# The last chunk pair of a ConvFFN's up projection as a block product, and the border to the down projection laid out anew

## The chip, the cores and the metric

The kernel runs on one core of one Trainium2 chip. Its engines run side by side and wait for one another by semaphores: PE (TensorE, the matrix multiplier), DVE (VectorE), ACT (ScalarE), POOL (GpSimd) and SP (SyncE, which here only issues DMAs). The metric is the device time of one execution in microseconds (us), as the median of several runs.

## The reference

One layer of a streaming encoder on 1024 positions plus 16 meta tokens, width 1024, all in float32. The work around the change is its last part, a gated feed-forward with a causal convolution of width 3, and a final norm:

```python
def _conv_ffn(xn, w_up, conv_w, conv_b, w_down):
    hid = xn @ w_up                       # (1040, 1024) @ (1024, 5632)
    hp = jnp.pad(hid, ((0, 0), (CONV_WIDTH - 1, 0), (0, 0)))
    conv = conv_b + sum(hp[:, j:j + seq_len] * conv_w[j] for j in range(CONV_WIDTH))
    val, gate = jnp.split(conv, 2, axis=-1)
    return (jax.nn.silu(gate) * val) @ w_down   # (1024, 2816) @ (2816, 1024)
```

## The kernel before

Every float32 operand of a matmul is held as two tiles, a rounded high part and the low rest. A cast (ACT, from raw to high) and a split (raw minus high, on DVE or POOL, the helper at line 137) make them, and each product is three matmuls: high by high, high by low, low by high.

**Up.** The hidden width of 2816 is 22 chunks of 128 (NFF); for each chunk c there is a gate chunk and a value chunk of weights, so a chunk pair. The normed input lies transposed in `xhi` and `xlo` (128 partitions, 8 rows of K, 1040 columns). Pairs 0, 1, 2 and 21 are *plain* (`plain_steps`, line 1339): for each half three pieces of about 342 columns, each 24 matmuls into one bank, then the convolution straight from the bank (ACT line 1361, DVE line 1363). Pairs 3 to 20 are *block pairs* (`block_pair`, line 1490): the four quarters of weights and input are combined to seven products in place of eight (`seven`, line 217). `weight_forms` makes the combined weights (POOL sums at line 1451, casts at 1304, splits at 137), and the combined inputs T1 to T4 stand in the pool `tforms` (the list `T`). A block pair reads B11, B21 and B22 of `xhi` and `xlo` and the four forms, in the order A11 B11, S2 T2, A12 B21, S3 T3, S1 T1, A22 T4, S4 B22, each in two pieces of 258 and 256 columns and 12 matmuls a piece. The quarter B12 is read only when the forms are made. A block pair's result goes through `hg` and `hv` (three buffers `h` in pool `hid`), and then through the convolution (ACT line 1501, DVE line 1503, twice for each half). `glue` (line 1311) does silu on ACT, the product of gate and value (POOL, for the last pair DVE), and the store to `a_d` in HBM.

**Down.** The product of `a_d` with `w_down` is made in the same seven-product way from 11 pairs of rows j, in four groups: (8, 9), (7, 0, 1), (2, 3, 4), (5, 6, 10). Each group runs seven products p in the order 0, 4, 1, 2, 5, 3, 6 (the last group differs), each over four row tiles, with three matmuls of 512 columns for each j. `forms(p, j)` (line 1561) loads a tile of weights (`wr`) and a tile of rows (`ar`), casts both and splits both, on POOL for p = 0, 4 and 5 and on DVE otherwise, into an operand slot from the list `ops`. p = 4, 5 and 6 accumulate in the banks of 0, 1 and 3, after these have been copied out (lines 1702 to 1707). The sums stand in `u2` and in the rows `hs`, whose first four tiles are loaded with the residual (`h_load`).

**The border.** The plain pair 21 needs no T forms, so their pool is closed before it, and down's first pool `down1` (operand slots, raw buffers `a00` to `a11` and eight weight buffers `w`) takes its bytes while the plain pair runs. When the up stage's pools close (`st_r`: weights ring, hidden rows, outputs), the second pool `down` takes theirs: `gfB`, raw buffers, `u2`, `hs`, two more slots. A tile that takes used bytes waits until the last reader of them is done.

What sets the order: the program is traced, and a scheduler at build time sets for each engine one fixed order of instructions, by readiness in its own model and program order. `after(a, b)` adds an edge that places a behind b. Each engine, and each engine's DMA queue, then works in its order; an instruction that waits holds everything behind it on its engine.

## Time and profile before

| | us |
|---|---|
| three runs | 1425.33, 1426.13, 1426.46 (median 1426.13) |
| the profiled execution | 1427.24 |
| its span, from the first to the last instruction | 1425.5 |
| block pairs c = 3 to 20 | 824.3 to 1183.9 |
| plain pair c = 21 | 1183.9 to 1206.6 |
| down, TensorE | 1206.6 to 1417 |
| last evictions, norm and stores | 1417 to 1425.5 |

Times inside the profile count from the first instruction. The profile gives for each engine its busy time, and for each instruction its start, its duration and what ended the idle time before it. A matmul's duration includes its way through the array, which the next matmul overlaps, so that TensorE's pace is read from start to start.

### The profile page before, as it was taken

How to read it: one execution, taken by the hardware profiler on the slowest of the kernel's cores; microseconds unless marked ns; L12 is line 12 of the kernel's file. 1: busy time of each engine (PE TensorE's matmuls, PEld its weight loads, DVE VectorE, ACT ScalarE, POOL GpSimd, SP SyncE). 2: the span in 40 equal slices, each digit the busy share in tenths (PEclk: the TensorE clock that was granted, in tenths of full speed). 3: DMA queues.
4: the chain of work that ended last, by engine and by line, in shares of the span. 5: the costliest groups of instructions: out<-in, count | busy, mean ns of one | idle time of the engine just before them, and what ended most of it. 6: DMA issues, size and time to landing. Idle time of an engine off the chain costs nothing.

```text
span 1425.5 us, 26319 instructions
## 1 busy us (share of the span) xinstructions
PE 1410.6 (99%) x9607; PEld 1336.1 (94%) x9607; DVE 1070.3 (75%) x2048; ACT 709.0 (50%) x1381; POOL 764.2 (54%) x872
## 2 busy tenths in 40 slices
...
PEclk9999999999999999999999999999999999999999
...
GB/s 298 176 203 147 160 106 133 172 119 31 53 156 161 127 111 57 23 287 267 216 161 124 73 114 183 183 173 177 178 142 113 98 79 258 327 205 133 129 94 118
DMA packets 93318, 216.17 MB, mean 152 GB/s; under 512 B 14802, under 2 KB 22610, under 8 KB 92804
## 3 DMA queue, kind: packets, MB, share of 16 engines
...
HBM read 170.88 MB, written 71.71 MB: 170 GB/s over the span
## 4 chain that ended last, share of the span: by engine, by line
PE 95%; DMA 2%; issue 1%; ACT 1%; DVE 0%; POOL 0%; POOLq 0%; DVEq 0%; SPq 0%
PE mm L174 5%; PE mm L176 5%; PE mm L175 5%; PE sp L236 4%; PE sp L237 4%; PE sp L238 4%; PE tp L236 3%; PE tp L237 3%; PE tp L238 3%; PE mm L238 3%; PE mm L236 3%; PE mm L237 3%; PE po L966 3%; PE tp L920 2%; PE mm L1699 2%; PE mm L1698 2%
## 5 line engine op out<-in xcount | busy, mean ns | idle before, releaser
L174 PE MATMUL mm<-xhi,whi 128*128 128x342 f32 (+2 forms) x480 | 156.1, 325 | 0.0
L175 PE MATMUL mm<-xlo,whi 128*128 128x342 f32 (+2 forms) x480 | 155.4, 324 | 0.0
L176 PE MATMUL mm<-xhi,wlo 128*128 128x342 f32 (+2 forms) x480 | 154.6, 322 | 0.5 <-DMA wlo<-in_w_g_dram 0.5
L1313 POOL TENSOR_TENSOR ov<-ov,og 128x1024 f32<-128x1024 f32 x21 | 50.8, 2421 | 119.7 <-ACT og L1312 117.4
L137 DVE TENSOR_TENSOR sw<-sf,sw 128x512 fp32r<-128x512 f32 x72 | 73.4, 1020 | 46.2 <-ACT sw L1304 45.1
L1304 ACT CAST sw<-sf 128x512 fp32r<-128x512 f32 x72 | 44.9, 624 | 108.9 <-POOL sf L1451 80.1
L176 PEld LDWEIGHTS mm<-xhi,wlo 128*128 128x128 f32 x480 | 90.4, 188 | 1.3 <-DMA wlo<-in_w_g_dram 0.8
L174 PEld LDWEIGHTS mm<-xhi,whi 128*128 128x128 f32 x480 | 90.4, 188 | 1.1 <-issue 0.6
L175 PEld LDWEIGHTS mm<-xlo,whi 128*128 128x128 f32 x480 | 90.4, 188 | 0.4
L1451 POOL TENSOR_TENSOR sf<-raw,sf 128x512 f32<-128x512 f32 x36 | 62.9, 1748 | 38.8 <-DVE sw L137 38.7
L1451 POOL TENSOR_TENSOR sf<-raw 128x512 f32<-128x512 f32 x36 | 49.1, 1363 | 60.0 <-ACT ov L1361 21.5
L238 PE MATMUL mm<-xhi,sw 128*128 128x258 f32 (+1 forms) x288 | 81.0, 281 | 0.0
L236 PE MATMUL mm<-xhi,sw 128*128 128x258 f32 (+1 forms) x288 | 80.8, 280 | 0.0
L237 PE MATMUL mm<-xlo,sw 128*128 128x258 f32 (+1 forms) x288 | 80.7, 280 | 0.0
L883 ACT ACTIVATE pt<-pt,mx 128x400 f32<-128x400 f32 (+5 forms) x72 | 53.1, 737 | 45.2 <-DVE mx L876 44.9
L1503 DVE SCALAR_TENSOR_TENSOR ov<-hv,cwt,ov 128x1024 f32<-128x1024 f32 x36 | 69.9, 1942 | 0.4 <-ACT ov L1501 0.4
L885 POOL TENSOR_SCALAR pt<-pt,mx 128x400 f32<-128x400 f32 (+5 forms) x72 | 51.8, 721 | 33.3 <-DVE mx L884 28.3
L1304 ACT CAST sw<-raw 128x512 fp32r<-128x512 f32 x70 | 43.0, 621 | 45.0 <-PE sp L238 23.1
L137 DVE TENSOR_TENSOR sw<-raw,sw 128x512 fp32r<-128x512 f32 x70 | 57.9, 831 | 4.3 <-ACT sw L1304 4.0
L137 DVE TENSOR_TENSOR tl<-tp,th 128x512 fp32r<-128x512 f32 (+1 forms) x80 | 50.7, 634 | 12.2 <-ACT th L923 11.6
L923 ACT CAST th<-tp 128x512 fp32r<-128x512 f32 (+1 forms) x80 | 43.4, 543 | 32.1 <-PE tp L920 22.7
L852 POOL CAST qz<-q 64x128 fp32r<-64x128 f32 (+1 forms) x72 | 20.2, 283 | 67.2 <-PE sp L871 65.7
...
## 6 DMA issues: line engine op xcount, KB each, us to landing
raw<-in_w_up_dram SPq DMA_DIRECT2D x44, 512.0 KB, 3.7
t_d<-in_w_dn_dram POOLq DMA_DIRECT2D x44, 256.0 KB, 6.9
wr<-t_d SPq DMA_DIRECT2D x44, 256.0 KB, 3.4
ar<-a_d SPq DMA_DIRECT2D x41, 256.0 KB, 5.3
a_d<-ov SPq DMA_DIRECT2D x18, 512.0 KB, 2.6
wr<-in_w_dn_dram SPq DMA_DIRECT2D x33, 256.0 KB, 3.8
t_d<-in_w_dn_dram SPq DMA_DIRECT2D x22, 256.0 KB, 4.3
t_d<-t_d SPq DMA_DIRECT2D x22, 256.0 KB, 4.7
```

The lines of the kernel that those rows point to most:

```text
L137: return eng.tensor_tensor(out_, src, hi.bitcast(F), ALU.subtract)
L174: yield PE.matmul(ps, whi[:, i, :], ahi[:, i], start=(i == 0), stop=False)
L175: yield PE.matmul(ps, whi[:, i, :], alo[:, i], start=False, stop=False)
L176: yield PE.matmul(ps, wlo[:, i, :], ahi[:, i], start=False, stop=(i == k - 1))
L236: PE.matmul(ps, a[0][:, i], bh, start=(i == 0 and not joins), stop=False, skip_group_check=True)
L237: PE.matmul(ps, a[0][:, i], bl, start=False, stop=False, skip_group_check=True)
L238: PE.matmul(ps, a[1][:, i], bh, start=False, stop=(i == kh - 1), skip_group_check=True)
L883: ends[:] = rd, S.activation(pt[:n, :kc], pt[:n, :kc], AF.Exp, bias=low, scale=-1.0, accum_out=nm[:n, 0:1])
L885: sc_.append(GP.tensor_scalar(pt[:n, :kc], pt[:n, :kc], nm[:n, 1:2], 1.0, ALU.mult, ALU.mult))
L1304: S.copy(hi, src)
L1451: sums.append(GP.tensor_tensor(f_, a, b, op))
L1503: V.scalar_tensor_tensor(out=o, in0=h_[:, j:SEQ + j], scalar=cwc(j, m), in1=o, op0=ALU.mult, op1=ALU.add)
```

## The change

Chunk pair 21 becomes a block pair like those before it. Since it reads the T forms, their pool now lives through it, and down's first tiles are placed by when bytes come free:

- a small pool `down0`, taken before the forms, holds two weight buffers, two raw buffers `a00` and the constant `eps`; the slots of p = 0 are the quarter B12 of `xhi` and `xlo`;
- `down1` takes the bytes of the forms, whose tiles are laid out in the order of their last use (T2, T3, T1, T4): six weight buffers, `a01`, two slots (p = 4), `a10`, `a11`, `hs` 0 to 3, `u2`; p = 1 and 2 take quarters (0, 0) and (1, 0) as slots;
- `down` takes the bytes of the up stage: `gfB`, the raw buffers of every second pair of rows, `hs` 7 and 6, two slots (p = 5), two more (p = 6), `hs` 5 and 4; p = 3 takes quarter (1, 1).

The convolution of pair 21 (`conv_pair`) is now traced behind down's first product. Edges set the order at the border: the loads of group 0 in a chain behind the last up weights, pair 20's store behind the eighth of them, the `hs` loads behind the sixteenth; casts of p = 0 behind the pair's copies of c1, of p = 4 ahead of the first evictions, of p = 6 behind p = 1's evictions; the gate half of the convolution behind p = 1's splits and the value half behind p = 2's; p = 4's additions behind the gate half. The last pair's store is issued by POOL's queue in place of ACT's, and its outputs take the usual output buffers in place of the hidden rows' buffers.

```diff
--- before.py
+++ after.py
@@ -211,6 +211,8 @@
             los.append(split_lo(V, dlo[:, 4 * hf:4 * hf + 4, col:col + n], t3[:, :, :n], ho))
         return los
 
+    kept = {}
+
     def m_ps():
         return pp.tile([P, 512], F, tag="mm", name="mm", bufs=3)
 
@@ -242,7 +244,7 @@
             V.tensor_tensor(to, a, b, ALU.add)
 
         for q in st:
-            S.copy(q["c1"], prod(q, "a", m_ps, A11, B11))
+            kept["c1"] = S.copy(q["c1"], prod(q, "a", m_ps, A11, B11))
         for q in st:
             add(q["u2"], prod(q, "b", s_ps, S2, T2), q["c1"])
         for q in st:
@@ -1292,7 +1294,7 @@
     after_of = {None: (1,), 0: (5,), 4: (2,), 5: (3, 6)}
     def up_raw(m):
         raw = rp.tile([P, KD, P], F, tag="raw", name="raw", bufs=3)
-        SY.dma_start(raw, w_up[m])
+        kept["raw"] = SY.dma_start(raw, w_up[m])
         return raw
 
     def ring():
@@ -1309,7 +1311,9 @@
         return cwt[:, j, m:m + 1]
 
     def glue(g_, v_, c):
-        S.activation(g_, g_, AF.Silu)
+        silu = S.activation(g_, g_, AF.Silu)
+        for cp_ in first_copy:
+            after(silu, cp_)
         (V if c == NFF - 1 else GP).tensor_tensor(v_, v_, g_, ALU.mult)
         l_, r_ = HALF
         rows = a_d[P * c:P * c + P]
@@ -1317,7 +1321,7 @@
             SY.dma_start(rows[:, l_], v_[:, l_])
             even[0] = v_
             return
-        (S if c == NFF - 1 else SY).dma_start(rows, v_)
+        kept[c] = (GP if c == NFF - 1 else SY).dma_start(rows, v_)
         if c // 2 not in SUMMED:
             return
         e_, j = even[0], c // 2
@@ -1328,12 +1332,10 @@
         for p, t_ in ((1, e_[:, l_]), (2, g_[:, l_]), (3, e_[:, r_]), (6, g_[:, r_])):
             SY.dma_start(s_d[p][P * j:P * j + P], t_)
 
+    first_copy, last_gate = [], []
     even, SUMMED = [None], (7, 8, 9)
 
     def conv_out(m, tag):
-        if m % NFF == NFF - 1:
-
-            return ha.tile([P, SEQ], F, tag="h", name=tag, bufs=3, padded_shape=[P, 2 * NH])
         return ha.tile([P, SEQ], F, tag=tag, name=tag, bufs=OUTS[tag])
 
     def plain_steps(c, parts=(QBLK,), ws={}):
@@ -1440,9 +1442,15 @@
     NH = LQ // 2 + 1
     HS = LQ - NH
     PIECES = [(0, 258), (258, 256)]
+    down0 = pool(ctx, "down0", side="left")
+    for tag in ("a00", "w"):
+        down0.tile([P, 512], F, tag=tag, name="hold", bufs=2)
+    eps = down0.tile([P, 1], F, name="eps")
+    V.memset(eps, EPS)
     st_t = ExitStack()
     tq = pool(st_t, "tforms", side="left")
-    T = [[tq.tile([P, KH, NH], R, name=f"t{i}{w}") for w in "hl"] for i in range(4)]
+    T = {i: [tq.tile([P, KH, NH], R, name=f"t{i}{w}") for w in "hl"] for i in (1, 2, 0, 3)}
+    T = [T[i] for i in range(4)]
 
     sums = []
 
@@ -1495,32 +1503,58 @@
         hg = ha.tile([P, LQ], F, tag="h", name="hg", bufs=3, padded_shape=[P, 2 * NH])
         hv = ha.tile([P, LQ], F, tag="h", name="hv", bufs=3, padded_shape=[P, 2 * NH])
         seven(ha, A, [B11, T3, T2, T1, B21, T4, B22], KH, PIECES, HS, hg, hv)
-        res = []
-        for h_, m, tag in ((hg, NFF + c, "og"), (hv, c, "ov")):
-            o = conv_out(m, tag)
-            S.activation(o, h_[:, :SEQ], AF.Identity, bias=cwc(3, m), scale=cwc(0, m))
+        return hg, hv
+
+    def conv_pair(c, hg, hv, behind=()):
+        res = {}
+        halves = ((hg, NFF + c, "og"), (hv, c, "ov"))
+        for h_, m, tag in halves:
+            res[tag] = o = conv_out(m, tag)
+            act = S.activation(o, h_[:, :SEQ], AF.Identity, bias=cwc(3, m), scale=cwc(0, m))
+            if behind:
+                after(act, casts[7])
             for j in (1, 2):
-                V.scalar_tensor_tensor(out=o, in0=h_[:, j:SEQ + j], scalar=cwc(j, m), in1=o,
-                                       op0=ALU.mult, op1=ALU.add)
-            res.append(o)
-        glue(*res, c)
+                st_ = V.scalar_tensor_tensor(out=o, in0=h_[:, j:SEQ + j], scalar=cwc(j, m), in1=o,
+                                             op0=ALU.mult, op1=ALU.add)
+                for cut in behind[:4] if tag == "og" else behind:
+                    after(st_, cut)
+                if tag == "og":
+                    last_gate[:] = st_,
+        glue(res["og"], res["ov"], c)
 
     run(first_pair)
     xn_forms()
     plain_pair(1)
     plain_pair(2)
     for c in range(3, NFF - 1):
-        block_pair(c)
-    st_t.close()
-    plain_pair(NFF - 1)
-
-
-
-    down1 = pool(ctx, "down1", side="left")
-    small = [down1.tile([P, 4, 512], R, name=f"op{q}") for q in range(4)]
-    ops = [[t_[:, w] for w in range(4)] for t_ in small]
-    ops += featq
-    dpool = {}
+        conv_pair(c, *block_pair(c))
+
+
+
+    def quarter(r, h_):
+        cols = slice((L - 512) * h_, (L - 512) * h_ + 512)
+        return [[t_[:, KH * r + 2 * q + w, cols] for w in range(2) for t_ in (xhi, xlo)] for q in range(2)]
+
+    ops = quarter(0, 1)
+    n_w = [0]
+
+    def weight_tile():
+        n_w[0] += 1
+        if n_w[0] % 8 in (1, 2):
+            return down0.tile([P, 512], F, tag="w", name="wr", bufs=2)
+        return down1.tile([P, 512], F, tag="w", name="wr", bufs=6)
+
+    def raw_buffer(j, tag):
+        pl = dpool[turn_of[j] % 4 // 2]
+        if pl is dpool[0] and tag == "a00":
+            pl = down0
+        return pl.tile([P, 512], F, tag=tag, name="ar", bufs=2)
+
+    def op_tiles(pl, q0, q1):
+        small = [pl.tile([P, 4, 512], R, name=f"op{q}") for q in range(q0, q1)]
+        return [[t_[:, w] for w in range(4)] for t_ in small]
+
+    dpool = {0: None}
     pairs = {}
     groups = [(8, 9), (7, 0, 1), (2, 3, 4), (5, 6, 10)]
     turn_of = {j: n for n, j in enumerate(j for grp in groups for j in grp)}
@@ -1529,19 +1563,25 @@
 
     def raw_tile(j, k, h_):
         if (k, h_) not in pairs.setdefault(j, {}):
-            pairs[j][k, h_] = dpool[turn_of[j] % 4 // 2].tile([P, 512], F, tag=f"a{k}{h_}", name="ar", bufs=2)
+            pairs[j][k, h_] = raw_buffer(j, f"a{k}{h_}")
         return pairs[j][k, h_]
 
+    first_loads = []
+
     def behind(ld, j):
-        if h_load and j in groups[1]:
+        if h_load and len(first_loads) == 16:
             after(ld, h_load[-1])
+        if j in groups[1]:
+            after(ld, first_loads[-1])
+        if j in groups[0]:
+            after(ld, first_loads[-1] if first_loads else kept["raw"])
+            first_loads.append(ld)
 
     LAST = NFF // 2 - 1
     FROM = {0: (0, 0), 4: (1, 0), 5: (1, 1)}
 
     def load_form(p, j):
-        t_ = dpool[turn_of[j] % 4 // 2].tile([P, 512], F, tag={0: "a00", 4: "a01", 1: "a10", 2: "a11", 5: "a00", 3: "a01", 6: "a10"}[p],
-                                    name="ar", bufs=2)
+        t_ = raw_buffer(j, {0: "a00", 4: "a01", 1: "a10", 2: "a11", 5: "a00", 3: "a01", 6: "a10"}[p])
         if p in FROM:
             k, h_ = FROM[p]
             c0 = P * (2 * j + k)
@@ -1559,7 +1599,7 @@
 
 
     def forms(p, j):
-        b_ = down1.tile([P, 512], F, tag="w", name="wr", bufs=8)
+        b_ = weight_tile()
         behind(SY.dma_start(b_, w_block(*own_w[p], j) if p in own_w else t_d[p][P * j:P * j + P]), j)
 
         if j not in SUMMED:
@@ -1581,18 +1621,32 @@
         eng = GP if p in (0, 4, 5) else V
         for q, src in ((0, a_), (2, b_)):
             hi = S.copy(slot[q], src)
+            if j in groups[0] and p == 0:
+                after(hi, kept["c1"])
+            elif j in groups[0]:
+                casts.append(hi)
+                if p in (3, 6):
+                    after(hi, casts[15])
+            elif j in groups[1] and p == 0:
+                after(hi, casts[15])
             if first_copy and j in groups[0] and p >= 5:
                 after(hi, first_copy[1])
             cut = split_lo(eng, slot[q + 1], src, slot[q])
             if eng is V:
                 cuts.append(cut)
+            if j in groups[0] and p == 6:
+                late_casts.append(hi)
+            elif j in groups[0] and p == 5:
+                fifth[:] = cut,
+            elif j in groups[1] and p == 0:
+                after(cut, fifth[0])
             if first_add and eng is V and j in groups[0] and p > 2:
                 after(cut, first_add[1 if p == 3 else 3])
             if eng is V and j in groups[-1] and p == 6:
                 after(cut, first_add[-1])
         return slot
 
-    first_add, first_copy, cuts = [], [], []
+    first_add, cuts, late_casts, fifth, casts = [], [], [], [], []
 
 
 
@@ -1687,7 +1741,7 @@
         bks = banks(g, p)
         for t, (c0, n) in parts:
             bk = held["end"] if last and p in (3, 6) and c0 else bks[t]
-            top, bot = hs[t], hs[4 + t]
+            top, bot = hs.get(t), hs.get(4 + t)
             to_, o = {0: (u2[t], 0), 1: (bot, 512), 2: (u2[t], 0), 3: (bot, 512),
                       4: (top, 0), 5: (bot, 0), 6: (top, 512)}[p]
             ts_ = slice(P * t, P * t + P)
@@ -1700,11 +1754,17 @@
             to = to_[:, o + c0:o + c0 + n]
             if first and p == 0:
                 first_copy.append(S.copy(to, ps))
+                after(first_copy[-1], casts[3])
             elif first and p in (1, 5):
 
-                S.activation(to, ps, AF.Copy, scale=-1.0 if p in MINUS else 1.0)
+                ev = S.activation(to, ps, AF.Copy, scale=-1.0 if p in MINUS else 1.0)
+                if p == 1:
+                    for hi in late_casts:
+                        after(hi, ev)
             else:
                 first_add.append(V.tensor_tensor(to, to, ps, ALU.subtract if p in MINUS else ALU.add))
+                if len(first_add) <= 4:
+                    after(first_add[-1], last_gate[0])
             if g == 2 and p == 3:
                 GP.dma_start(bot, h_d[P * (4 + t):P * (4 + t) + P], accum_op=ALU.add)
             if last and p == 6:
@@ -1749,25 +1809,40 @@
                         load_pair(j)
             ready[g, p] = [forms(p, j) for j in groups[g]]
 
+    last_pair = block_pair(NFF - 1)
+    ready[0, 0] = [forms(0, j) for j in groups[0]]
+    st_t.close()
+    down1 = pool(ctx, "down1", side="left")
     dpool[0] = down1
-    for p in ORDER[:2]:
+    down1.tile([P, 512], F, tag="w", name="hold", bufs=6)
+    down1.tile([P, 512], F, tag="a01", name="hold", bufs=2)
+    small = op_tiles(down1, 0, 2)
+    for tag in ("a10", "a11"):
+        down1.tile([P, 512], F, tag=tag, name="hold", bufs=2)
+    hs = {c: down1.tile([P, D], F, name=f"hs{c}") for c in range(4)}
+    u2 = [down1.tile([P, 512], F, name=f"u2{c}") for c in range(4)]
+    ops += small + quarter(0, 0) + quarter(1, 0)
+    for p in (4, 1, 2):
         ready[0, p] = [forms(p, j) for j in groups[0]]
+    after(kept[NFF - 2], first_loads[7])
+    for c in range(4):
+        h_load.append(SY.dma_start(hs[c], h_d[P * c:P * c + P]))
+        after(h_load[-1], first_loads[-1])
+    product(0, 0, ready[0, 0], True, False)
+    conv_pair(NFF - 1, *last_pair, behind=cuts)
     st_r.close()
     dn = pool(ctx, "down", side="left")
     dpool[1] = dn
     gfB = dn.tile([P, D], F, name="gfB")
-    dn.tile([P, 512], F, tag="a00", name="hold", bufs=2)
+    for tag in ("a00", "a01", "a10", "a11"):
+        dn.tile([P, 512], F, tag=tag, name="hold", bufs=2)
+    hs.update((c, dn.tile([P, D], F, name=f"hs{c}")) for c in (7, 6))
     sq = dn.tile([P, 512], BF, name="sq")
-    eps = dn.tile([P, 1], F, name="eps")
-    V.memset(eps, EPS)
-    u2 = [dn.tile([P, 512], F, name=f"u2{c}") for c in range(4)]
-    hs = [dn.tile([P, D], F, name=f"hs{c}") for c in range(4)]
-    hs += [dn.tile([P, D], F, name=f"hs{c}") for c in range(4, KD)]
-    small2 = [dn.tile([P, 4, 512], R, name=f"op{q}") for q in range(4, 6)]
-    ops += [[t_[:, w] for w in range(4)] for t_ in small2]
-    for c in range(4):
-        h_load.append(SY.dma_start(hs[c], h_d[P * c:P * c + P]))
-    for g, p in turns:
+    ops += op_tiles(dn, 2, 4) + quarter(1, 1) + op_tiles(dn, 4, 6)
+    hs.update((c, dn.tile([P, D], F, name=f"hs{c}")) for c in (4, 5))
+    cuts.clear()
+    ops += ready[0, 0]
+    for g, p in turns[1:]:
         prepare()
         if (g, p) == (1, 0):
             SY.dma_start(gfB, gf.partition_broadcast(P))
```

## The prediction

> **What bounds the kernel now.** I read the page first: busy shares, the slices, the chain of work that ended last.
>
> ```profile
> span 1425.5 us, 26319 instructions
> PE 1410.6 (99%) x9607; PEld 1336.1 (94%) x9607; DVE 1070.3 (75%) x2048; ACT 709.0 (50%) x1381; POOL 764.2 (54%) x872
> PEclk9999999999999999999999999999999999999999
> PE 95%; DMA 2%; issue 1%; ACT 1%; DVE 0%; POOL 0%; POOLq 0%; DVEq 0%; SPq 0%
> ```
>
> TensorE is the bound, at its full granted clock; every other engine only has to be in time. The averages don't say whether that holds at the border, so the timeline of TensorE comes next, at four places: the start of the last block pair (c=20), of the plain pair (c=21), of down, and of down's second group of row pairs. The first column is the start.
>
> ```profile
> 1163.95 0.28 PE L236 MATMUL mm<-xhi,sw 128*128 128x258 f32 x1
> 1164.07 0.28 PE L237 MATMUL mm<-xlo,sw 128*128 128x258 f32 x1
> ...
> 1183.93 0.32 PE L1357 MATMUL mm<-xhi,sw 128*128 128x344 f32 x1
> 1184.09 0.33 PE L1358 MATMUL mm<-xlo,sw 128*128 128x344 f32 x1
> ...
> 1206.63 0.40 PE L1697 MATMUL mm<-op 128*128 128x512 f32 x1
> ...
> 1244.81 0.39 PE L1697 MATMUL sp<-op 128*128 128x512 f32 x1
> ```
>
> A matmul's duration overlaps the next one; what counts is from start to start. The stretches between those starts:
>
> ```profile
> core 0: us, PE busy (x) PEld busy (x) DVE busy (x) ACT busy (x) POOL busy (x), PEclk, DMA share, GB/s
> 1163.95:1183.93 19.98, 19.98 (x170) 19.98 (x169) 11.87 (x19) 7.59 (x13) 6.81 (x5) 1.00 0.29 102
> 1183.93:1206.63 22.70, 22.70 (x146) 22.70 (x145) 13.91 (x19) 13.60 (x22) 15.69 (x9) 1.00 0.79 282
> 1206.63:1244.80 38.17, 38.17 (x170) 31.54 (x169) 28.89 (x36) 24.41 (x47) 26.39 (x18) 1.00 0.91 329
> ```
>
> The border holds no idle time of TensorE that could be won. All there is to win is the matmul work of one chunk pair.
>
> **The change part by part.** *The plain pair becomes a block pair.* A plain pair is 144 matmuls (2 chunks x 3 pieces x 24) and took 22.70 us, 0.158 us each. A block pair is 168 matmuls (7 products x 2 pieces x 12) of 258 or 256 columns and took 19.98 us, 0.119 each. TensorE saves 22.70 - 19.98 = **2.72 us**. The form has a price on the other engines: seven casts and seven splits of weights in place of four, and four sums on POOL. They fall beside the pair before, where the row of 1163.95 shows DVE 11.87, ACT 7.59 and POOL 6.81 of 19.98 us busy: cost nothing. Were the cover gone, DVE would be the first to fill.
>
> The Trainium skill, TensorE: Matmul & The Clock Gate, section "Back-to-back issue gap", gives columns/2.4 + 2.5 ns at full clock. As an estimate from it, a plain pair is 144 x 145.3 = 20.9 us, a block pair 168 x 109.6 = 18.4, the gain 2.5. The trace's spacings lie 8% above it, and the sum goes by the trace.
>
> *What has to be in time.* With the pair starting at 1183.93, its seven products of 2.85 us end at 1186.8, 1189.6, 1192.5, 1195.3, 1198.2, 1201.1 and 1203.9. Down's products of group 0 are 38.17/7 = 5.45 us each, so p = 0, 4, 1, 2, 5, 3, 6 must start at 1203.9, 1209.4, 1214.8, 1220.3, 1225.7, 1231.2 and 1236.6, and group 1 at 1242.1. The prices of what feeds them, by groups of instructions (mean ns after the bar) and by DMA issues (us to landing), both of 1160 to 1262:
>
> ```profile
> L137 POOL TENSOR_TENSOR op<-wr,op 128x512 fp32r<-128x512 f32 x10 | 16.8, 1686 | 6.0 <-ACT op L1583 6.0
> L1583 ACT CAST op<-wr 128x512 fp32r<-128x512 f32 x16 | 9.6, 619 | 1.1 <-DMA wr<-in_w_dn_dram 1.1
> L137 DVE TENSOR_TENSOR xhi<-ar,xhi 128x512 fp32r<-128x512 f32 x6 | 5.3, 885 | 2.7 <-PE mm L1359 2.4
> L1503 DVE SCALAR_TENSOR_TENSOR og<-hg,cwt,og 128x1024 f32<-128x1024 f32 x4 | 6.3, 1568 | 0.8 <-ACT og L1501 0.7
> L1707 DVE TENSOR_TENSOR hs<-hs,mm 128x512 f32<-128x512 f32 x9 | 6.1, 679 | 8.0 <-PE mm L1699 8.0
> ...
> ar<-a_d SPq DMA_DIRECT2D x27, 256.0 KB, 5.9
> wr<-t_d SPq DMA_DIRECT2D x20, 256.0 KB, 5.4
> hs<-h_d SPq DMA_DIRECT2D x4, 512.0 KB, 5.2
> a_d<-ov ACTq DMA_DIRECT2D x1, 512.0 KB, 2.6
> ```
>
> *p=0* goes to a quarter of xhi and xlo that no block product reads, and its raw buffers no longer wait for the up stage's bytes. Its casts stand behind the pair's c1 copies (about 1187): 4 casts and 4 splits on POOL at 1.69 us end at 1194.4, 9 us early.
>
> *p=4* takes its weight and row buffers from the bytes of the form T2, read last at 1189.6. 5.9 us of landing, 2.5 of casts, then four splits on POOL, behind p=0's and c=20's product of 2.4 us: about 1205. With every split as long as a slow one just before down (2.27 us, below) it is 1208. Needed at 1209.4: hidden. SP's queue stops at p=4's first load until 1189.6, and at p=1's row tile until T1's bytes are free (1198.2). Behind it stand c=20's store, which nobody needs before the last group, and the hs loads.
>
> *p=1 and p=2.* From 1198.2 SP has 7 loads of 256 KB and 4 of 512 KB, then the 12 of p=5, 3 and 6: 7 MB, 18 us at the 392 GB/s below. p=1's operands land by 1205, p=2's by about 1207, hs by 1213, p=5's by 1216. DVE then has, in the order that the new edges set, p=1's four splits, the two gate convolutions, p=4's four adds, and p=2's four splits: 8 x 0.885 + 2 x 1.568 + 4 x 0.679 = 12.9 us, from 1205.5 to 1218.4, for p=2 at 1220.3. Cover 1.9 us, the thinnest at the border. Both ends, from the rows below: splits at 0.69 and convolutions at 1.27 give 10.8 us, cover 4; splits at 1.78 and convolutions at 2.20 give 21.4, a stall of 6.6. I take the middle, since POOL, whose work goes with the long splits, has done p=4 by then and waits for p=5's loads. The rows are from the timeline (start, us), one line's durations (minimum/median/maximum, ns) and the stretches:
>
> ```profile
> 1203.61 0.69 DVE L137 TENSOR_TENSOR xhi<-ar,xhi 128x512 fp32r<-128x512 f32 x1 [2.39 <-PE mm L1359]
> ...
> 1228.07 1.78 DVE L137 TENSOR_TENSOR op<-ar,op 128x512 fp32r<-128x512 f32 x1
> ...
> L1503 DVE SCALAR_TENSOR_TENSOR og<-hg,cwt,og x36: 1268/1272/2201, 847.6 to 1188.9; 128x1024 f32<-128x1024 f32 x36
> ...
> 1185.48 2.27 POOL L137 TENSOR_TENSOR op<-ar,op 128x512 fp32r<-128x512 f32 x1
> ...
> 1192.20 1.29 POOL L137 TENSOR_TENSOR op<-wr,op 128x512 fp32r<-128x512 f32 x1
> ...
> 1190.00:1196.00 6.00, 6.00 (x40) 6.00 (x40) 3.28 (x5) 2.70 (x5) 6.00 (x5) 1.00 1.05 392
> ```
>
> The Trainium skill, SBUF — State Buffer, section "Who interferes with whom", says that a VectorE instruction with two SBUF inputs and a GpSimd one that reads SBUF exclude each other, the second standing until the first ends. The trace agrees in kind: the same split takes 0.69 us with POOL idle and 1.78 beside it.
>
> *p=5, 3, 6* go to bytes of the weight ring and of the last block. p=5's loads land by 1216 and its four splits end at 1223 for 1225.7. p=1's copies into hs4 to hs7 need the bytes of the up weights and the gate's hidden rows, free before 1219. Nothing.
>
> *The last convolution* moves from beside TensorE's plain pair to behind product p=0. Its value half comes after all eight splits: two convolutions at 1.57 and the product of 1.23 (below) end at 1222.8, and the store, now issued by POOL, lands 2.6 us later at best and, with a split of 2.27 ahead of it and 6.9 for landing (the POOL queue's row), at 1232. Nobody waits for its data before the last group; its bytes are another matter, and are the third rival.
>
> *The end* (1416.85 on) is unchanged: nothing. The constant eps and the order of the T tiles: nothing.
>
> Sum: 2.72 us and no stall. The profiled execution took 1427.24 us, 1.74 beyond its span, and gives 1424.5. It lay 1.11 above the median of the three runs; against 1426.13 the forecast is **1423.4 us**.
>
> **The rivals.** *DVE's queue becomes the bound at p=2.* For it: the slow splits above, and DVE already 28.89 of 38.17 us busy there before four convolutions and a product move in. Against: its adds gate p=2 tile by tile, 1.36 us apart, and POOL has a pause. Bounds 0 to 6.6 us of stall; the likeliest when it happens is the half of it that one engine's overlap gives, 2 us: 1425.4.
>
> *It gives nothing.* p=4's chain from T2's bytes could lose the 2.7 us that the pair wins: with c=20's product also late and all eight POOL splits at 2.27, 1208 becomes 1212. Time 1426.1. Against: POOL's splits take 1.29 us where DVE reads PSUM (1192.20).
>
> *The last store holds group 1: slower.* The raw row buffers of the second pool lie on the bytes of the last convolution's outputs. The same thing is in the trace of before: the hs loads stood behind the store of ov.
>
> ```profile
> SPq L1769 <- DMA a_d<-ov: 7.2, 1, 7.2
> ...
> 1211.28 1.23 DVE L1313 TENSOR_TENSOR ov<-ov,og 128x1024 f32<-128x1024 f32 x1
> ...
> 1216.52 2.94 SPq L1558 DMA_DIRECT2D ar<-a_d x6
> ...
> 1234.07 3.01 POOL L137 TENSOR_TENSOR op<-wr,op 128x512 fp32r<-128x512 f32 x2
> 1237.04 1.74 POOL L1570 TENSOR_TENSOR ar<-ar 128x512 f32<-128x512 f32 x1
> ...
> t_d<-in_w_dn_dram POOLq DMA_DIRECT2D x44, 256.0 KB, 6.9
> ```
>
> Group 1's loads were issued from 1216.52 and its p=0 splits ended at 1237.1: 20.6 us, 7.7 ahead of TensorE. Now they can go only when the store has landed, 1225.4 to 1232. If all of them stand behind it, less the 4 us that the hs loads took in between, the splits end at 1242 to 1248.6 for 1242.1: a stall of 0 to 6.5. It decides from a landing of 1225.5 on. The price at its end is 6.5: 1429.9. Against: only tiles on those bytes wait, the weights and the first pool's tiles can pass, and one late tile needs 5.9 + 0.62 + 1.69 = 8.2 us, 1240 from a landing at 1232.
>
> **How the numbers follow.** Two measurements of this kernel tell apart about 0.2%, 2.85 us; a gain of 2.72 is just inside that. No stall (1423.4): 0.60. DVE's queue (1425.4): 0.17. Nothing (1426.1): 0.06. The store (to 1429.9): 0.17. Faster by over 0.2% needs 1423.28 or less: with the three runs 1.1 us apart, 4 in 10 of the first case, 0.24. Slower by over 0.2%, above 1428.98, needs a stall above 5.6: most of the last case and the upper end of the second, 0.14. The rest, 0.62, is within. The range begins at 1422.6, the gain and half the runs' spread with a little of TensorE's spacing, and reaches to 1427.8, a stall of 4.4 us: about 0.05 is left out below and 0.15 above. The likeliest case alone is 1422.6 to 1424.2.
>
> **What would show it.** TensorE's first matmul of down 19.98 us behind the pair's first, not 22.70, and group 1 some 58.2 us behind the pair's start. p=4's last POOL split before 1209.4; p=2's last DVE split before 1220.3, else the first rival: TensorE's gap then follows a DVE split or add. A gap ahead of group 1's first matmul, ended by an ACT or POOL form whose load stood behind the store, is the third rival. I am wrong altogether if a block pair at the border takes more than 20 us, or if TensorE idles before 1203.9.

## The result, and the profile after

| | us |
|---|---|
| before, four runs beside those of after | 1426.3 (1425.33 to 1427.49) |
| after, four runs | 1439.79 (1439.05 to 1445.14) |
| ratio | 1.0102, 95% interval 1.0077 to 1.0128 |
| span of the profiled execution, before and after | 1425.5 and 1437.9 |

The forecast was 1423.4, with a range up to 1427.8. The change costs 13.5 us. In the kernel after, line numbers are shifted: down's matmuls are L1751 to L1753, the down forms' casts L1623, the convolution on DVE L1517, the product of gate and value L1317, the store L1324, the adds L1765, the loads of pairs of rows L1598.

From the page of after, the head, the busy times and the clock granted to TensorE in 40 slices of the span, in tenths. The averages hardly differ from before's; the 8 in the clock's row is the slice that holds the border:

```profile
span 1437.9 us, 26381 instructions
PE 1412.7 (98%) x9631; PEld 1334.0 (93%) x9631; DVE 1085.9 (76%) x2053; ACT 712.4 (50%) x1384; POOL 775.4 (54%) x877
PEclk9999999999999999999999999999999999899999
```

The border by stretches of 6 us, after. Columns: stretch, its length, then busy time (instructions) of PE, PEld, DVE, ACT and POOL, the granted clock, the DMA share and GB/s:

```profile
1202.00:1208.00 6.00, 6.00 (x33) 5.07 (x32) 1.44 (x3) 2.73 (x6) 1.30 (x1) 1.00 1.03 394
1208.00:1214.00 6.00, 6.00 (x28) 4.92 (x27) 2.89 (x4) 6.00 (x11) 0.00 (x0) 1.00 1.04 396
1214.00:1220.00 6.00, 6.00 (x28) 4.91 (x27) 6.00 (x9) 3.13 (x6) 0.00 (x0) 1.00 1.04 382
1220.00:1226.00 6.00, 6.00 (x27) 4.59 (x25) 6.00 (x9) 6.00 (x13) 0.68 (x2) 1.00 0.15 50
1226.00:1232.00 6.00, 0.65 (x2) 0.19 (x1) 6.00 (x2) 2.21 (x5) 6.00 (x5) 0.92 0.68 215
1232.00:1238.00 6.00, 0.00 (x0) 0.00 (x0) 6.00 (x3) 2.97 (x5) 5.99 (x6) 0.50 0.73 259
1238.00:1244.00 6.00, 5.94 (x19) 4.78 (x20) 6.00 (x5) 1.57 (x4) 6.00 (x4) 0.72 0.70 247
```

TensorE does nothing for two stretches, and the clock granted to it falls to 0.50. Ahead of that POOL has nearly nothing for three stretches, and in the fourth the DMA drops from 382 to 50 GB/s. The busy share of DVE says 6.00, but with two instructions where nine were usual. The timeline of after shows what they are (start, us, engine, line, operation, tiles, in brackets the idle time before and who ended it):

```profile
1183.13 0.28 PE L238 MATMUL mm<-xhi,sw 128*128 128x258 f32 x1
1203.10 0.40 PE L1751 MATMUL mm<-xhi 128*128 128x512 f32 x1
...
1226.26 0.49 PE L1751 MATMUL po<-xhi 128*128 128x512 f32 x1
1238.06 0.79 PE L1752 MATMUL mm<-xlo,xhi 128*128 128x512 f32 x1 [11.31 <-DVE xlo L137]
...
1239.07 0.63 PE L1752 MATMUL mm<-xlo,xhi 128*128 128x512 f32 x1
1239.50 0.63 PE L1753 MATMUL mm<-xhi,xlo 128*128 128x512 f32 x1
...
1217.81 0.68 DVE L137 TENSOR_TENSOR xlo<-ar,xhi 128x512 fp32r<-128x512 f32 x1
...
1223.79 1.21 DVE L1317 TENSOR_TENSOR ov<-ov,og 128x1024 f32<-128x1024 f32 x1
...
1226.12 10.20 DVE L137 TENSOR_TENSOR xlo<-ar,xhi 128x512 fp32r<-128x512 f32 x1
1236.25 1.75 DVE L137 TENSOR_TENSOR xlo<-wr,xhi 128x512 fp32r<-128x512 f32 x1
...
1205.88 1.30 POOL L137 TENSOR_TENSOR op<-ar,op 128x512 fp32r<-128x512 f32 x1 [6.11 <-ACT op L1623]
1225.31 0.63 POOL L1324 DMA_DIRECT2D a_d<-ov  x1 [18.13 <-DVE ov L1317]
1225.95 1.28 POOL L137 TENSOR_TENSOR op<-ar,op 128x512 fp32r<-128x512 f32 x1
...
1230.86 2.47 POOL L137 TENSOR_TENSOR xlo<-wr,xhi 128x512 fp32r<-128x512 f32 x2
1233.30 4.15 POOL L137 TENSOR_TENSOR xlo<-ar,xhi 128x512 fp32r<-128x512 f32 x3
...
1219.84 0.62 ACT L1623 CAST op<-wr 128x512 fp32r<-128x512 f32 x1
...
1218.52 12.46 SPq L1598 DMA_DIRECT2D ar<-a_d  x5
```

And in the chain of work that ended last (start, us, what), the store's transfer:

```profile
1225.31 4.86 DMA a_d<-ov
```

And what SP's queue waits for between 1205 and 1245 (us in total, times, longest):

```profile
SPq L1598 <- DVE ov L1317: 6.1, 1, 6.1
...
SPq L1598 <- DMA a_d<-ov: 4.3, 1, 4.3
```

Read from below: the store lands at 1230.2. SP's queue needs 12.46 us for five loads of group 1, since their bytes are those of the last convolution: 6.1 us go by until DVE's product is done with them, and 4.3 more until the store is. POOL stands 18.13 us in front of that same store, which waits for DVE's product of 1223.79. Behind it stand p=5's splits, whose casts were done by 1220.5; they and those of group 1 then run one behind the other, eight at about 1.24 us, and for just that time DVE is held in one split of 0.69 us' work: 10.20 us. It is p=3's. TensorE's order for group 0 is here 0, 4, 1, 2, 3, 5, 6, with p=3 ahead of p=5, so p=3 is needed at 1225.2. After the stall the matmuls stand 0.43 us apart until 1241.5.

Where the 12.4 us between the two spans are: TensorE starts the last pair 0.8 us sooner, and the pair takes 2.7 less; down takes 226.85 us from its first matmul to its last for 210.43, 16.4 more; the tail gives back 0.5. Of the 16.4, 14.0 are gaps and matmuls at the low clock: the sum, over all starts more than 0.26 us apart, of what they take beyond the usual distance. The other 2.4 lie in the cadence of all the rest of down's 942 matmuls: 0.2303 us from start to start for 0.2276, in the mean over those of 512 columns. In a window without a gap, the count of TensorE's instructions in 120 us shows it. The row of before (stretch, length, TensorE's busy time and instructions, clock, DMA share, GB/s):

```profile
1280.00:1400.00 120.00, 120.00 (x528) 1.00 0.39 106
```

The same row of after, six fewer in the same time:

```profile
1280.00:1400.00 120.00, 120.00 (x522) 1.00 0.45 130
```

### The profile page after: what moved, and what is told of

Its sections match the earlier page's. It is cut to its first block, busy times and chain, and to the rows that moved or that the text cites. A ratio compares the mean times of both kernels' runs of the same rounds, so it can differ in the third digit from the quotient of the medians.

```text
span 1437.9 us, 26381 instructions
## 1 busy us (share of the span) xinstructions
PE 1412.7 (98%) x9631; PEld 1334.0 (93%) x9631; DVE 1085.9 (76%) x2053; ACT 712.4 (50%) x1384; POOL 775.4 (54%) x877
## 3 DMA queue, kind: packets, MB, share of 16 engines
q8 instruction: 76, 1.25, 0.4%
## 4 chain that ended last, share of the span: by engine, by line
PE 86%; issue 5%; POOL 3%; DVE 3%; DMA 2%; ACT 1%; SPq 0%; POOLq 0%; DVEq 0%
PE mm L174 6%; PE mm L175 6%; PE mm L176 6%; PE sp L238 4%; PE sp L239 4%; PE sp L240 4%; PE po L968 3%; PE mm L240 2%; PE mm L239 2%; PE mm L238 2%; PE tp L238 2%; PE tp L239 2%; PE tp L240 2%; PE tp L922 2%; PE mm L1753 1%
## 5 line engine op out<-in xcount | busy, mean ns | idle before, releaser
L137 DVE TENSOR_TENSOR sw<-sf,sw 128x512 fp32r<-128x512 f32 x76 | 78.6, 1034 | 47.1 <-ACT sw L1306 46.8
L1317 POOL TENSOR_TENSOR ov<-ov,og 128x1024 f32<-128x1024 f32 x21 | 50.9, 2422 | 115.0 <-ACT og L1314 112.6
L1459 POOL TENSOR_TENSOR sf<-raw,sf 128x512 f32<-128x512 f32 x38 | 67.3, 1772 | 39.4 <-DVE sw L137 39.3
L240 PE MATMUL mm<-xhi,sw 128*128 128x256 f32 (+1 forms) x304 | 85.5, 281 | 0.0
L238 PE MATMUL mm<-xhi,sw 128*128 128x256 f32 (+1 forms) x304 | 85.3, 281 | 0.0
L239 PE MATMUL mm<-xlo,sw 128*128 128x256 f32 (+1 forms) x304 | 85.3, 280 | 0.0
L1517 DVE SCALAR_TENSOR_TENSOR ov<-hv,cwt,ov 128x1024 f32<-128x1024 f32 x38 | 71.6, 1884 | 0.0
```

Of the source, the lines that this page charges most:

```text
L137: return eng.tensor_tensor(out_, src, hi.bitcast(F), ALU.subtract)
L238: PE.matmul(ps, a[0][:, i], bh, start=(i == 0 and not joins), stop=False, skip_group_check=True)
L239: PE.matmul(ps, a[0][:, i], bl, start=False, stop=False, skip_group_check=True)
L240: PE.matmul(ps, a[1][:, i], bh, start=False, stop=(i == kh - 1), skip_group_check=True)
L1459: sums.append(GP.tensor_tensor(f_, a, b, op))
L1517: st_ = V.scalar_tensor_tensor(out=o, in0=h_[:, j:SEQ + j], scalar=cwc(j, m), in1=o, op0=ALU.mult, op1=ALU.add)
```

## The experiments

The time of before beside each group of runs was 1425.85, 1426.26, 1426.58, 1427.08 and 1426.69 us. "Gaps" is the sum over down as above. In store_on_act and store_on_sp, in the four runs that only move slots, and in early2_wait beside early2, TensorE, DVE, ACT and POOL keep their order of work. In the others the scheduler set another order, above all for group 1, so part of their change in time can come from that.

### Moving the store

At first three things stood against each other: that the store's wait holds the forms behind it, and POOL's run then keeps DVE out (H); that the store's queue alone matters (Q); and that DVE has more to do behind 1212 than time to do it (D). **store_on_act** and **store_on_sp** move the one instruction:

```diff
-        kept[c] = (GP if c == NFF - 1 else SY).dma_start(rows, v_)
+        kept[c] = (S if c == NFF - 1 else SY).dma_start(rows, v_)    # store_on_act
+        kept[c] = SY.dma_start(rows, v_)                             # store_on_sp
```

> The last pair's store is issued by ACT's queue as before the change; PE, DVE and SP keep their order. Theory H (a store that waits in an engine's queue holds what is behind it; when it lets go, POOL runs its late splits without a gap and DVE's split, which TensorE needs, stands until they are through): the wait only moves. On ACT the store stands ahead of p=5's casts, so POOL still gets its splits late and in a row: a DVE split of over 5 us, a stall of TensorE of 8 to 14 us, 1436 to 1446 us. Rival D (DVE's queue is simply too long at the border, whoever issues the store): the same stall, 1437 to 1441 us. Rival Q (it is the cost of a DMA issued by POOL): the stall goes, 1424 to 1428 us.

> The last pair's store is issued by SP's queue; PE, DVE and ACT keep their order. Theory H: POOL's wait of 18 us is gone, p=5's splits run from about 1218 on, no DVE split above 5.1 us (the longest in the profile of before, beside four POOL splits in a row), TensorE stalls at most 5 us: 1428 to 1433 us. Rival D: DVE still comes to p=3's splits at 1226 and TensorE stalls 8 us or more: 1436 us and up. The forecast's third rival (group 1's loads behind the store): a stall ahead of group 1, and none at p=3.

ScalarE's queue: 1435.13 us, ratio 1.0063 (1.0048 to 1.0078), gaps 9.0. SP's: 1436.44, 1.0071 (1.0056 to 1.0086), gaps 8.7. So the long stall goes, and with it 3 to 4 of the 13.5 us, no more (9.3 and 10.6 over before are left). With the store on ScalarE's queue the wait moved as H has it: ScalarE stands 7.05 us in front of the store, p=5's splits begin at 1226.02 and p=3's at 1228.06, and TensorE's longest wait, 3.3 us, is for a cast of ScalarE. But no DVE split at the border lasts over 1.79 us there, so H's second half did not come, and the time lies outside all three ranges. With the store on SP's queue p=5's splits run from 1220.38 to 1228.07, the time is above H's range, and D has it. What TensorE waits for in store_on_sp between 1203 and 1280 (waiting engine and line, who ended it, us in total, times, longest):

```profile
PE sp L1751 <- DVE u L1765: 2.7, 2, 1.9
PE mm L1752 <- DVE xlo L137: 2.1, 2, 1.8
```

Everything it waits for there is DVE's, splits and then adds, and no DVE instruction at the border lasts over 1.8 us. That spoke for DVE's amount of work. **sp_no_shift** puts the constant eps at the end of the last pool as well, so that the tiles of down start at multiples of 64 bytes as before.

> The store on SP and the constant eps (32 bytes) taken from the small pool ahead of the forms to the end of the last pool, so that the forms, down's buffers and the slots stand on multiples of 64 bytes as before. It asks why down's matmuls of 512 columns stand 0.2303 us apart after the change and 0.2276 before. If the shift is the cause: 0.2276 again and 942 x 0.0027 = 2.5 us less than with the store on SP alone. If not: 0.230, and the same time within 1 us.

1435.14, 1.0063 (1.0048 to 1.0078), spacing 0.2309: the shift that the constant makes is not what widens the cadence. **pool_rests** leaves the store and breaks POOL's run:

```diff
+            rest = GP.tensor_copy(rest_, slot[q][:, :1].bitcast(F)) if eng is GP and (j in groups[0] and p == 5 or j in groups[1] and p == 0) else None
             cut = split_lo(eng, slot[q + 1], src, slot[q])
+            if rest is not None:
+                after(cut, rest)
```

> The kernel after, with a copy of one element on POOL ahead of each of the splits of p=5 in group 0 and of p=0 in group 1; the store stays on POOL. Theory H in its second half (a row of splits without a gap is what keeps DVE out): POOL still waits 18 us for DVE, but DVE gets in between the splits: no DVE split above 2.5 us there, a stall of 3 to 6 us, 1430 to 1435 us. If the row does not matter, or a rest this short leaves no gap: a DVE split of 8 us or more and 1438 to 1441 us.

1442.03, 1.0113 (1.0096 to 1.013): a miss by both. DVE's split took 5.80 us in place of 10.20 and the gap there 6.3 in place of 11.8, but another of 4.5 came at 1265 and the clock fell twice. A one-element instruction between two splits doesn't let DVE in: POOL's splits keep their 1.25 us through four of them. (The run is of four there, and not of eight, because POOL then stands 2.25 us for a cast.)

### The convolution back to its place, and the spacing

**conv_early** calls it right behind the last pair, value half first:

```diff
     last_pair = block_pair(NFF - 1)
+    conv_pair(NFF - 1, *last_pair)
...
-    conv_pair(NFF - 1, *last_pair, behind=cuts)
```

> The changed kernel with the last convolution back right behind the last block pair, value half first and without the edges that hold it behind p=4's casts and the eight splits; the store stays on POOL. Theory H+D (the stall is DVE's border work compressed into 1212 to 1238, because the edges leave DVE idle some 6.7 us before 1212, and POOL held by the store until 1225): DVE's convolutions lie in 1200 to 1210, POOL's gap ahead of the store shrinks from 18 us to under 8, TensorE's gaps in down fall from 14 us to under 3, 1424 to 1428. The spacing of down's matmuls should stay at 0.230 (theory L, the layout), which by itself takes 2.5 us back, so that H+D with L gives 1425.5 to 1428. Rival (the border has too little room whatever the order, DVE's load being over its time even with its idle time used): TensorE still waits 6 us or more for a DVE split or add between 1220 and 1265, 1432 or above.

1434.14, 1.0059 (1.0047 to 1.0072), gaps 9.7. That is 7.9 over before, 5.6 better than after, and well short of the 1424 to 1428 expected; the time lies where the rival had it, at 1432 or above. The timeline of conv_early:

```profile
1202.51 1.24 ACT L1515 ACTIVATE ov<-hv,cwt 128x1024 f32<-128x1024 f32 x1 [8.67 <-DVE hv L244]
...
1210.68 2.28 POOL L137 TENSOR_TENSOR op<-ar,op 128x512 fp32r<-128x512 f32 x1
1216.15 0.63 POOL L1324 DMA_DIRECT2D a_d<-ov  x1 [3.19 <-DVE ov L1317]
1216.80 1.30 POOL L137 TENSOR_TENSOR op<-ar,op 128x512 fp32r<-128x512 f32 x1
...
1216.37 6.02 DVE L137 TENSOR_TENSOR xlo<-wr,xhi 128x512 fp32r<-128x512 f32 x1
```

The store holds POOL for 3.19 us only, but ScalarE now stands 8.67 us in front of the convolution with p=4's casts behind, so p=4's last split ends at 1213; and p=5's four splits keep DVE out again, now from p=2's. The gap ahead of p=2 is 3.3 us; it ends as the first of p=4's adds, which stand behind these splits, is over (1224.8; the profile names a cast that ended with it). One held engine went for another.

The spacing was tried in the same group. **conv_early_quarters** moves the quarters' columns so that the parts of a slot (high and low of the rows and of the weights) lie at multiples of 512 bytes from each other; **before_wide_slots** does the reverse to the kernel before, and **before_store_on_pool** gives it the change's place of the store alone:

```diff
-        cols = slice((L - 512) * h_, (L - 512) * h_ + 512)
+        cols = [slice(512 * h_ + s, 512 * h_ + s + 512) for s in (16, 0)]     # conv_early_quarters
...
-    small = [down1.tile([P, 4, 512], R, name=f"op{q}") for q in range(4)]
+    small = [down1.tile([P, 4, 528], R, name=f"op{q}")[:, :, :512] for q in range(4)]     # before_wide_slots
...
-        (S if c == NFF - 1 else SY).dma_start(rows, v_)
+        (GP if c == NFF - 1 else SY).dma_start(rows, v_)     # before_store_on_pool
```

> As the kernel with the early convolution, and the four quarter slots of the last block forms moved by 16 columns in every other row, so that the four parts of a slot lie 4096 bytes apart instead of 4160, with the constant eps at the end of the last pool. Theory L (the distance between the parts of a slot sets the cadence): the spacing of down's 512-column matmuls goes from 0.2303 us back to 0.2276 or at least half of the way, and the time is 1.3 to 2.6 us below the kernel with the early convolution. Rival (the spacing comes from something else, such as the traffic or the place of the other tiles): spacing 0.2300 to 0.2305 and the same time within 0.6 us.

> The kernel before, with the parts of its six operand slots 2112 bytes apart instead of 2048; nothing else. Theory L: the matmuls of the products that read these slots stand 0.230 or more apart instead of 0.2276, and the time rises by 0.8 to 2.6 us, 1427 to 1428.8. Rival: spacing 0.2274 to 0.2278 and the same time within 0.5 us.

> The kernel before with only its last store on POOL's queue, as the change has it. Theory H+D (the store costs only where something that is needed soon stands behind it, and the convolution is late): in before POOL has no form from 1199 to 1215 and the convolution is early, so the same time within 1 us. Rival (the POOL queue is a bad place for the store in itself): 1428 or above.

conv_early_quarters: 1434.73, 1.0057 (1.0044 to 1.0071), spacing 0.2305: no cure. before_wide_slots: 1428.28, 1.0014 (1.0005 to 1.0022), 2.0 us and spacing 0.2299, as the layout theory has it. before_store_on_pool: 1426.28, 1.0001 (0.9993 to 1.001): the store on POOL's queue costs nothing where the convolution is early and nothing needed stands behind it.

### The order of the products, and POOL's reads

**fifth_before_third** and **early_fifth_first** put p=5 ahead of p=3 on TensorE, in after and in conv_early:

```diff
+                if first and p == 3:
+                    after(mm_, kept["mm5"])
```

> The changed kernel with one edge more: TensorE takes group 0's product p=5 before p=3, as the kernel before does; in the changed kernel p=3 stands ahead of p=5, so that its DVE splits are needed 5.5 us sooner. Theory O (the order of the products is a part of the loss): TensorE needs p=5 at 1225.2, has its first POOL splits at about 1228.4, and p=3's first two DVE splits at about 1238 for 1234: gaps of 3 to 4 and of 3 to 5 us instead of one of 11.8, less of the low clock, and 1433 to 1436.5. Rival (the sum of DVE's and POOL's work sets it, whatever the order): the gaps before group 1 still come to 11 us or more, and 1438 to 1441.

> The kernel with the early convolution, and p=5 ahead of p=3 on TensorE. There p=5's POOL splits were done 20 us ahead of their product, while p=3's DVE splits were 6.9 us late. Theory O: the gap of 2.67 us ahead of p=3 and the stretch at the low clock behind it go, the one of 3.27 us within p=2 (behind a DVE split of 6.0 us beside four POOL splits) stays: 1429 to 1432. Rival: a gap of the same size comes at p=6 or at group 1, 1433 or above.

1443.56, 1.0116 (1.0103 to 1.013), and 1435.64, 1.0062 (1.0049 to 1.0074): theory O missed in both. In the first the long DVE split stays (10.27 us), the gaps are 15.3, which is the rival's mechanism, and the time is above the rival's range as well. In the second, which the rival has at 1433 or above, the gap ahead of p=3 went from 2.7 to 0.9 us as forecast, and two of 1.8 and 1.6 came behind DVE adds at 1245 and 1250. The order of p=3 and p=5 alone wins nothing.

> As the one before it, and p=5's four POOL splits stand behind p=2's last DVE split, so that POOL has no run of splits while DVE makes p=1's and p=2's. Theory H (DVE stands still for as long as POOL runs splits one behind the other): no DVE split over 2 us before 1224, the gap within p=2 falls from 3.27 us to under 1, p=5's splits still end ahead of 1228, and all gaps come to under 3 us: 1425.5 to 1428.5, which is before's time within 0.2%, since the wider spacing of 0.2303 takes 2.5 of the pair's 2.72 us back. Rival (p=2's operands are late for another reason, loads or casts): a gap of 2.5 us or more within p=2, 1430 or above.

That edge set only the order in which the program is put together, and gave the same program; its 1435.2 (1.0061, 1.0048 to 1.0073) repeats early_fifth_first and says nothing of what it was to test. **pool_writes_zeros** lets POOL write where it would have read and written:

```diff
+            if j in groups[0] and p == 5 or j in groups[1] and p == 0:
+                cut = GP.memset(slot[q + 1].bitcast(F), 0.0)
```

> The changed kernel with POOL's splits of group 0's p=5 and group 1's p=0 replaced by writes of zeros into the same low parts: the low parts of these two products are left out, POOL reads nothing there, and every order and wait is as in the changed kernel. Theory H (DVE is kept out by POOL's reads): DVE's split of 10.20 us falls under 2 us, the gap of 11.80 us to under 4.5, no stretch at the low clock, 1428 to 1432. Rival D (DVE's amount of work behind 1212 is what makes p=3 late): the gap stays at 7 us or more, 1434 or above.

1437.25, 1.0076 (1.0062 to 1.009), gaps 11.4. At p=3 theory H has it: the long split is gone and the gap of 11.8 with it (1.2 left). The time is the rival's, 1434 or above: it is still 10.7 us over before. The timeline of pool_writes_zeros tells why:

```profile
1224.72 6.45 SPq L1598 DMA_DIRECT2D ar<-a_d  x5
...
1225.80 0.69 DVE L137 TENSOR_TENSOR xlo<-ar,xhi 128x512 fp32r<-128x512 f32 x1
...
1241.94 1.78 DVE L137 TENSOR_TENSOR xlo<-wr,xhi 128x512 fp32r<-128x512 f32 x1 [8.78 <-ACT xhi L1623]
...
1258.53 0.79 PE L1755 MATMUL sp<-op 128*128 128x512 f32 x1 [5.93 <-DVE u L1769]
```

DVE's split beside POOL's writes lasts 0.69 us. But SP still waits for the product and for the store to land (6.1 and 4.3 us, as in after), group 1's loads come late, DVE has nothing for 8.78 us, its adds come late behind late splits, and TensorE waits 5.93 us at 1252. So a second wait lay behind the first. (DVE's order differs from after's there by one split of group 1, put ahead; what that adds was not tried.) The theory that remained: several waits in a row, each hidden by the one ahead.

### Several waits together

**early2** has the convolution ahead of the first down product, its ScalarE steps behind p=4's first casts, and p=5 ahead of p=3. **early2_wait** adds a true wait (a semaphore, not only an order) of p=5's splits for p=2's, **early2_zeros** adds to early2 the zeros instead, and **zeros_no_store** takes from pool_writes_zeros the last store:

```diff
+    conv_pair(NFF - 1, *last_pair)
     product(0, 0, ready[0, 0], True, False)
-    conv_pair(NFF - 1, *last_pair, behind=cuts)
...
-            if behind:
-                after(act, casts[7])
+            if c == NFF - 1:
+                after(act, casts[3])
...
+            if j in groups[0] and p == 5:
+                wait_for(cut, kept["cut2"])     # early2_wait
```

> The changed kernel with the last convolution ahead of the first down product, its ScalarE steps behind p=4's first casts (in the kernel with the early convolution they stood ahead of them and held p=4's splits until 1213), no edges to the splits, and p=5 ahead of p=3 on TensorE. Theory S (several waits in a row): p=4's splits end ahead of 1208 and its gap of 0.7 us goes; DVE's split of about 6 us beside p=5's four POOL splits stays, with a gap of 2 to 3.5 us within p=2; 1431 to 1435. Rival N (one thing not yet named holds all of these kernels): 1434 to 1437 whatever is taken away.

> As early2, and p=5's POOL splits wait by a semaphore for p=2's last DVE split (the edge of the run early_fifth_first_apart set only the order in which the program was put together, and that program is the same as early_fifth_first's). Theory S: no DVE split over 2 us ahead of p=2's end, the gap within p=2 under 1 us, p=5's splits end at about 1225 for 1230, and 2 to 4 us less than early2: 1428 to 1432. Rival (the long split only moves on to p=3's splits, or POOL's later work is late in its turn): within 1 us of early2.

> As early2, with POOL's splits of group 0's p=5 and group 1's p=0 replaced by writes of zeros (these low parts are left out). Convolution early, order as before, nothing that keeps DVE out: Theory S: all gaps of TensorE in down come to under 3.5 us, 1426.5 to 1430. Rival N: gaps of 7 us or more and 1433 or above.

> As pool_writes_zeros, and the store of the last product left out; its rows in the tensor of products are filled from the chunk before, whose store is issued twice, so the result of the last chunk is left out. In pool_writes_zeros SP stood from 1225.1 to 1229.9, when the store landed, with group 1's loads behind it, DVE then had nothing for 8.8 us, and TensorE a gap of 6.3 us behind a late add. Theory S (the third wait): SP's stand and DVE's idle time shrink by 4 to 5 us, the gap of 6.3 falls under 3, and the time to 1430 to 1434. Rival N: the gap and the time stay, 1436 to 1438.

| | us | ratio, 95% interval | gaps |
|---|---|---|---|
| early2 | 1432.65 | 1.0040 (1.0028 to 1.0053) | 5.8 |
| early2_wait | 1430.70 | 1.0027 (1.0017 to 1.0038) | 4.3 |
| early2_zeros | 1430.18 | 1.0023 (1.0014 to 1.0032) | 4.4 |
| zeros_no_store | 1431.83 | 1.0030 (1.0018 to 1.0043) | 5.1 |

By the time three fell where the row of waits puts them, though the gaps at p=2 in early2 came to 1.4 us, not 2 to 3.5; early2_zeros lies 0.2 above its bound, with gaps of 4.4 for 3.5. Rival N, one cause behind all, would have left them above 1433. zeros_no_store also frees POOL, so that the 5.9 us by which it stands nearer to before than pool_writes_zeros are not the landing's alone. The pair early2 and early2_wait differs in one wait; their intervals overlap, so the 2 us between them are not clear of noise, and what the wait does is read from the traces. The timeline of early2 at p=2's splits:

```profile
1216.17 6.03 DVE L137 TENSOR_TENSOR xlo<-wr,xhi 128x512 fp32r<-128x512 f32 x1
...
1216.60 1.30 POOL L137 TENSOR_TENSOR op<-ar,op 128x512 fp32r<-128x512 f32 x1
```

And that of early2_wait (the helper of the splits is line 141 there):

```profile
1215.08 0.68 DVE L141 TENSOR_TENSOR xlo<-ar,xhi 128x512 fp32r<-128x512 f32 x1
...
1216.88 0.67 DVE L1779 TENSOR_TENSOR hs<-hs,po 128x512 f32<-128x512 f32 x1
...
1215.30 1.63 POOL L141 TENSOR_TENSOR op<-ar,op 128x512 fp32r<-128x512 f32 x1 [0.41 <-issue]
1216.88 1.31 POOL L141 TENSOR_TENSOR op<-wr,op 128x512 fp32r<-128x512 f32 x1
```

With the wait p=2's splits are over at 1215.8 in place of 1222.8 (down begins 1.7 us earlier in this profile). POOL's run falls beside adds that read PSUM, which last 0.67 us each, and TensorE has no gap up to 1236. What is left, in the waits of early2_wait between 1203 and 1280:

```profile
PE po L1761 <- DVE hs L1779: 1.3, 1, 1.3
PE mm L1761 <- DVE hs L1779: 1.0, 1, 1.0
PE sp L1761 <- DVE u L1779: 0.7, 2, 0.5
```

Adds again, between splits of 1.78 us beside POOL's of 1.75; that these splits make the adds late was not tried. Before had no room there either: from 1238 to 1262 its DVE is busy throughout, in the stretches of before

```profile
1238.00:1244.00 6.00, 6.00 (x28) 4.92 (x27) 6.00 (x7) 1.22 (x3) 6.00 (x5) 1.00 1.05 383
...
1256.00:1262.00 6.00, 6.00 (x28) 4.99 (x27) 6.00 (x5) 3.49 (x8) 6.00 (x4) 1.00 0.59 190
```

and TensorE has no gap all the same, since the work came in time.

### The spacing again

**early2_wait_2048** makes the distances between the parts of every slot multiples of 2048 bytes, as in before; **before_2560_slots** breaks that in four slots of before and keeps multiples of 512:

```diff
+    xp.tile([P, 384], F, name="apart")     # early2_wait_2048, with the columns as above
     xlo = xp.tile([P, KD, L], R, name="xlo")
...
-    small = [down1.tile([P, 4, 512], R, name=f"op{q}") for q in range(4)]
+    small = [down1.tile([P, 4, 640], R, name=f"op{q}")[:, :, :512] for q in range(4)]     # before_2560_slots
```

> As early2_wait, with the quarters' columns moved by 16 in every other row, 1536 unused bytes between the two tiles of forms and the constant eps in the last pool, so that the hi and lo parts of every slot lie at multiples of 2048 bytes from each other; from one slot to the next the distance is still 128 in every 512. Theory L2 (multiples of 2048 within the slot are what the cadence needs): spacing 0.2276 to 0.2290 instead of 0.2305 and 1.4 to 2.7 us less than early2_wait, 1427.5 to 1429.5. Rival (the distance from slot to slot, or something else, sets it): 0.2300 to 0.2306 and within 0.8 us of early2_wait.

> The kernel before, with the parts of its first four operand slots 2560 bytes apart instead of 2048: still multiples of 512, no longer of 2048. Theory L2: the matmuls of these four slots stand 0.230 or more apart, the whole of down 0.2285 or more, and 0.8 to 2 us are lost, 1427.5 to 1429. Rival (multiples of 512 are enough, and what cost the 2.0 us with slots of 2112 were the 64 bytes): spacing 0.2274 to 0.2280 and within 0.6 us of before.

early2_wait_2048: 1430.46, 1.0021 (1.0012 to 1.0031), spacing 0.2306. before_2560_slots: 1426.38, 0.9998 (0.9989 to 1.0007), spacing 0.2276. Both went as the rivals have it. The same window as above, first of before_wide_slots:

```profile
1280.00:1400.00 120.00, 120.00 (x523) 1.00 0.38 106
```

And of before_2560_slots, which has before's count:

```profile
1280.00:1400.00 120.00, 120.00 (x529) 1.00 0.38 106
```

So within a slot multiples of 512 bytes are enough. A pitch of 2112 costs 2.0 us, nearly what the changed kernel loses in cadence, and does so at before's traffic of 106 GB/s. The changed kernel's slots, even when aligned within, lie at odd multiples of 64 or 128 bytes from each other; whether that distance from slot to slot is the cause was not tried alone, and stays open. No version was found that is faster than before.

## Why the prediction was wrong, step by step

**The pair.** Right to 0.01: 1183.13 to 1203.10 is 19.97 us for 19.98, and TensorE does not stand until down begins. The gain of 2.72 is there.

**p=0, p=4, p=1, p=2.** In time, as predicted. p=4's last POOL split ended at 1207.2, inside the 1205 to 1208 given, 1.5 us ahead. p=2's last DVE split ended at 1218.5 (1217.81 and 0.68 above) for the 1218.4 of the sum. That agreement is luck: DVE began with these splits at 1207.2 and not at 1205.5, stood 3.2 us between them for casts, its splits took 0.69 and not 0.885 (POOL stood all the while), and only one of p=4's four adds came ahead of the last split. The cover was 1.2 for 1.9. The first rival did not come at p=2; its sign, a gap of TensorE behind a DVE split, came at p=3.

**"p=5's loads land by 1216 and its four splits end at 1223."** This is the step that failed. The splits began at 1225.95 and ended at 1230.9. The prediction moved the last store to POOL's queue and costed its landing, to 1232, and who needs its data and its bytes; it reckoned with a split ahead of the store and did not ask what stands behind it in POOL's order while it waits for DVE's product. It had that product's end 2.2 us early (two convolutions and the product "end at 1222.8"; 1225.0 measured). POOL stood 18.13 us, p=5's and group 1's splits were pushed into one run, and the run met p=3's splits on DVE. The step was late in a second way: ScalarE's casts of p=5 ended only at 1220.5, behind the silu, and with POOL free (store_on_sp) the splits still ended at 1228.07. And the prediction kept before's order, with p=5 due at 1225.7 and p=3 at 1231.2, where the program has p=3 first.

**"With splits at 1.78."** The upper bound for a DVE split beside POOL was taken from one row. The trace of before held a longer one, off the critical path, in its timeline:

```profile
1288.66 5.13 DVE L137 TENSOR_TENSOR op<-ar,op 128x512 fp32r<-128x512 f32 x1
...
1289.41 1.35 POOL L137 TENSOR_TENSOR op<-ar,op 128x512 fp32r<-128x512 f32 x1
1290.65 1.34 POOL L137 TENSOR_TENSOR op<-wr,op 128x512 fp32r<-128x512 f32 x1
1291.91 1.34 POOL L1574 TENSOR_TENSOR ar<-ar 128x512 f32<-128x512 f32 x1
```

The rule that the prediction cites from the Trainium skill (SBUF — State Buffer, section "Who interferes with whom"), that the second stands until the first ends, gives one POOL instruction of 1.3 us. The rows show a run: with eight in a row, 10.20.

**The third rival, group 1's loads behind the store's bytes.** The wait was there as described, and the landing (1230.2, inside 1225.4 to 1232). It was priced alone, at 6.5 at most, with no stall ahead of it. In the changed kernel the stall at p=3 covered it. With that gone it came forth, not ahead of group 1's first matmul, where the prediction looked for it, but inside group 1 behind a late add of DVE; without the store, and with POOL free, another 5.9 us went (from 10.7 over before's time of its group to 4.8).

**The spacing.** That down's matmuls keep 0.2272 was assumed without a word, since the products are the same. It is 0.2303 with the new slots, 2.4 us in all, and that alone takes nearly the whole gain back. before_wide_slots shows that the layout of the slots can do this; that it does it here, and which distance, was not shown.

**The sum.** 2.7 won; 2.4 lost in the cadence; 14.0 in gaps and low clock. That most of the gaps are those of a row of waits is shown by the runs: over the time of before in their own groups, after stands at 13.5, the early convolution at 7.9, early2 at 5.6, early2_wait at 3.6 us. Of the last, 4.3 of gaps and 2.7 of spacing stand against the 2.7, which makes 4.3; its interval is 2.4 to 5.4. What makes those last 4.3 us of gaps stays open.
